# Causal linear attention without carried states, and a rearranged last expert group and final store

## The chip, the cores and the metric

One NeuronCore of a Trainium2 chip runs the whole kernel. The metric is the device time of one execution in microseconds (us), from launch to the end; lower is better. Engines are named as in the profile: PE (TensorE matmul), PEld (TensorE weight load), DVE (VectorE), ACT (ScalarE), POOL (GpSimd), SP (the queue that issues the loads).

## The reference, cut to what matters

One decoder layer over 256 tokens of 1024 features, in float32: adaptive norm, a mixer of two branches (gated linear attention and a short gated convolution), then 64 experts in 8 groups, each token going to two experts of one group, then a last RMSNorm. What the change touches is the linear attention and the last norm:

```python
b = jnp.cumsum(gc, axis=3)                    # per chunk of 64 tokens; gc = log of the forget gate
q_t = qc * jnp.exp(b); k_t = kc * jnp.exp(-b); k_s = kc * jnp.exp(b_last - b)
attn = jnp.where(causal, einsum('nbhid,nbhjd->nbhij', q_t, k_t), 0.0)
o_intra = einsum('nbhij,nbhjv->nbhiv', attn, vc)
decay = jnp.exp(b_last)[:, :, :, 0, :]
def step(state, inp):                          # scan over the 4 chunks, 4 heads
    q_i, k_i, v_i, d_i = inp
    o_i = einsum('bhid,bhdv->bhiv', q_i, state)
    state = d_i[..., None] * state + einsum('bhid,bhiv->bhdv', k_i, v_i)
    return state, o_i
o = o_intra + o_inter
...
x = x + g2 * hier_moe(h)
return rmsnorm(x, final_norm_g)
```

There are 4 heads with 128 key features and 256 value features each, and 4 chunks of 64 tokens.

## The kernel before, in words

The weights are read once, 475.8 MB in all, in a fixed order through SP. The mixer's weights come as blocks of 512 KB into a ring of 12 (class Stream): 88 blocks of the input and output projections ("win") and 48 of the modulation ("modw"). A block is freed when DVE has read it, and the free issues the next load, so the ring runs as far ahead as DVE lets it. After the last block, the same ring and the buffers that the mixer gives up take "units" of 2 MB: 8 groups of 12 units of expert weights ("ew"; for the last group's second layer "el"). A unit's buffer is freed, and the next load issued, when PE has used it.

In the mixer every weight block is split by ACT (L340, high part) and DVE (L347, low part) into two float32r halves, and PE multiplies it in three passes (L356, 24 matmuls a block, or L364 and L373 for the first 16 blocks). The splits run 5 blocks ahead of PE. DVE also reduces a modulation block against the conditioning vector (L257); the table MODS says at which block each of these falls. What else the mixer does is hung on block numbers by at, first and pre: in block b, "first" comes before the splits, "pre" after them, "at" last before the block's matmuls. Each engine works its instructions in that order.

The linear attention hangs on blocks 16 to 46. Gate values give the running sum bb; its exponentials eb, enb and ekb weight the keys and queries (k_evac, q_evac). Then, on PE: the weighted keys are transposed (L481), attention within pairs of chunks is formed with a mask that leaves out the pair's second-chunk-on-first part (L494, DVE L498), the keys by the values give what each chunk adds to the state (L506), which ACT and DVE chain into three states (L513, L515), and the output of a head is attention times values (L525) plus query times state (L529). The output is normed per head; L556 spreads the four heads' norms over partitions with a matrix P1 that holds a row of ones per head (P1 is used again for the experts' slot tables).

An expert group's 4 experts run side by side in four column groups of PE, 32 tokens each (L1048). The last group's second layer is cut into four column chunks (LASTC: 512, 256, 128, 128) so that the work behind the last weights is short. Each chunk goes through last_part: scale out of PSUM (evac_y, L1066), spread the slots back to tokens on PE (combine, L1075) and add (L1079), square and sum on ACT (L1214), then last_weigh multiplies by the last norm's gain (L1218). At the end the sums give the norm's factor (L1241 to L1244), and four stores of 256 KB write the result. LASTN says in how many pieces the load of each chunk's weights is issued.

All four chunks accumulate in one PSUM tile ps of two banks: columns 0 to 511 in the first, all others in the second. A DMA issue on SP waits for an earlier DMA: the issues of the last pieces stand on the landings of earlier ones.

The places that the change touches:

```python
first(22, gate5); first(23, gate8); at(23, gate7)
at(27, gla_kst); at(28, gla_attn); first(28, gla_kst2); pre(29, gla_attn2, 0); pre(29, gla_attn2, 1)
at(29, gla_state, 0, 1); first(30, gla_state2, 0); pre(30, gla_state2, 1); at(31, gla_state, 2); pre(32, gla_state2, 2)
at(33, gla_o, 0) ... first(34, gla_o2, 0) ... at(36, gla_ss) ... at(39, gla_ss4)
```

Of the kernel before, what the change touches and what calls it, by code (L numbers as in the profile page):

```python
# [28 lines left out]
LASTN = (2, 2, 4, 4)  # L29
# [5 lines left out]
MODS = (16, 17, 18, 19, 22, 26, 27, 28, 31, 33, 34, 35, 37, 39, 41, 43, 45, 47, 49, 51, 52, 53, 54, 55, 56, 57, 58,  # L35
# [82 lines left out]
def trunk_kernel(ctx: ExitStack, tc: tile.TileContext, xT: bass.AP, c: bass.AP, modw: bass.AP,  # L118
# [113 lines left out]
    V.memset(cmask[0:64, 64:128], 0)  # L232
# [15 lines left out]
    G.memset(P1, 0.0)  # L248
    for h in range(H):
        G.memset(P1[32 * h:32 * h + 1, h // 2, h % 2], 1.0)  # L250
# [157 lines left out]
    la, bb, eb, enb = (t9[:, i].rearrange("p (h t) -> p h t", h=H) for i in range(4))  # L408
# [3 lines left out]
    ekb, qt, kt_, ks = (gb[:, i] for i in range(4))  # L412
    decay = sm.tile([128, H, 4], F32, name="decay")
    b4 = bb.rearrange("p h (c t) -> p (h c) t", t=64)
# [37 lines left out]
    def gate5():  # L452
        S.activation(eb, bb, AF.Exp, scale=-1.0 / 16)

    def gate6():
        V.tensor_sub(ekb.rearrange("p h (c t) -> p (h c) t", t=64),
                     b4[:, :, 63:64].to_broadcast([128, 16, 64]), b4)

    def gate7():
        V.tensor_copy(decay, eb.rearrange("p h (c t) -> p h c t", t=64)[:, :, :, 63])  # L460

    def gate8():
        S.activation(enb, bb, AF.Exp, scale=1.0 / 16)
        S.activation(ekb, ekb, AF.Exp, scale=-1.0 / 16)
# [3 lines left out]
    def gla_setup():  # L468
        g2 = big.tile([128, 4, 1024], F32, name="gc", tag="T11")
        L["kst"] = g2[:, 0].rearrange("p (t d) -> p t d", t=2)  # L470
        L["at"] = g2[:, 1].rearrange("p (t h i) -> p t h i", t=2, h=H)
        for ch, i in ((1, 2), (2, 3), (3, 0)):
            L["S", ch] = g2[:, i].rearrange("p (h d) -> p h d", h=H)
        G.memset(g2[:, 1], 0.0)

    def gla_kst():
        L["pk"] = []
        for tt in range(TT):
            ps = mt(H, 128)
            for h in range(H):  # L480
                T.transpose(ps[:, h], ks[:, h, 128 * tt:128 * tt + 128], ident)  # L481
            L["pk"].append(ps)

    def gla_kst2():
        for tt in range(TT):
            S.copy(L["kst"][:, tt], fl(L["pk"][tt]))

    def gla_attn():
        L["pa"] = []
        for tt in range(TT):  # L490
# [9 lines left out]
    def gla_state(*chs):  # L500
        for ch in chs:
            L["ps", ch] = [mt(2, 256) for _ in range(2)]
# [818 lines left out]
```

## Time and profile before

| | us |
|---|---|
| median of 3 runs (lowest, highest) | 1206.16 (1203.33, 1206.17) |
| profiled execution, its own time | 1202.4 |
| its span, first to last instruction | 1200.5 |
| PE busy | 903.8 (75%) |
| DVE busy | 381.6 (32%) |
| ACT busy | 224.6 (19%) |
| HBM read | 475.79 MB, 397 GB/s over the span |
| chain that ended last | DMA 67%, PE 28%, DVE 3% |

The shares of busy time are averages over three stages: the mixer to about 292 us, the eight expert groups to about 1180 us, and the tail behind the last weights. The chain of waits says who set the time in each: PE in the mixer, the load stream in the expert groups, and a chain that hops between PE, DVE and ACT in the tail.

### The profile page before, as it was taken

To read this page: it belongs to the slowest core of one execution; us is meant where nothing else is said; L and a number is where in the kernel's file an instruction comes from. 1 tells how busy PE (TensorE), PEld (TensorE's weight loads), DVE (VectorE), ACT (ScalarE), POOL (GpSimd) and SP (SyncE) were. 2 spreads that over 40 slices of the span, in tenths; PEclk is the share of its full clock that TensorE was granted. 3 is DMA by queue.
4 is the path that set the end of the run, shared out by engine and by line. 5 is a ranking of instruction groups with operands and counts; after the bars stand their busy time and mean duration, and the time that the engine had idled before them with its cause. 6 is when DMAs were issued, how large, how long until landed. Compare 5 with 4: busy or idle time off the path is not lost.

```text
span 1200.5 us, 14607 instructions
## 1 busy us (share of the span) xinstructions
PE 903.8 (75%) x6188; PEld 476.8 (40%) x6188; DVE 381.6 (32%) x720; ACT 224.6 (19%) x375; POOL 3.9 (0%) x15
## 2 busy tenths in 40 slices
PE   9999999999888766666666667676667566756575
PEld 6999999999342212121212212121212111412112
DVE  8968699664431111111111101020202000302103
ACT  6775545443210101010101000000000000100002
POOL 0000000000000000000000000000000000000000
PEclk9999999999998888798788888788888886989888
DMA  9987589979999999999999999999999999999996
GB/s 369 396 339 254 177 300 339 381 271 364 421 430 430 429 432 431 430 431 430 430 432 430 429 432 430 430 432 429 431 431 430 431 430 431 428 432 431 429 428 261
DMA packets 51483, 477.84 MB, mean 398 GB/s; under 512 B 5971, under 2 KB 6099, under 8 KB 27093
## 3 DMA queue, kind: packets, MB, share of 16 engines
q1 hardware_dynamic: 50544, 475.81, 95.8%
q8 instruction: 50, 0.82, 0.2%
q10 hardware_dynamic: 868, 1.05, 0.2%
q14 instruction: 21, 0.16, 0.0%
HBM read 475.79 MB, written 1.05 MB: 397 GB/s over the span
## 4 chain that ended last, share of the span: by engine, by line
DMA 67%; PE 28%; DVE 3%; ACT 0%; issue 0%; DVEq 0%; SPq 0%; ACTq 0%
DMA unit<-in_ew_dram 45%; DMA ring<-in_ew_dram 19%; PE z L356 17%; PE a L1048 3%; DMA unit<-in_el_dram 2%; PE m L364 2%; PE z L373 2%; PE m L1020 1%; PE m L1075 1%; PE m L529 0%; DMA xt<-in_xT_dram 0%; PE z L220 0%; PE m L506 0%; PE m L525 0%; PE m L312 0%
## 5 line engine op out<-in xcount | busy, mean ns | idle before, releaser
L1048 PE MATMUL a<-unit,xt 128*32 128x512 f32 x1440 | 209.5, 711 | 103.9 <-DMA unit<-in_ew_dram 103.9
L1048 PE MATMUL a<-unit,gt 128*32 128x512 f32 x736 | 121.7, 799 | 63.5 <-DMA unit<-in_ew_dram 59.9
L1048 PEld LDWEIGHTS a<-unit,xt 128*32 128x32 f32 x1440 | 43.8, 120 | 248.2 <-DMA unit<-in_ew_dram 139.0
L356 PE MATMUL z<-hhl,sp 128*128 128x256 f32 x1152 | 140.9, 284 | 0.0
L356 PEld LDWEIGHTS z<-hhl,sp 128*128 128x128 f32 x1152 | 138.9, 192 | 1.6 <-issue 1.5
L1024 ACT ACTIVATE xt<-m,modc,A 128x128 f32<-128x128 f32 x64 | 25.9, 453 | 518.5 <-PE m L1020 517.4
L347 DVE TENSOR_TENSOR sp<-ring,sp 128x1024 fp32r<-128x1024 f32 x88 | 106.8, 1219 | 40.2 <-ACT sp L340 40.1
L1048 PE MATMUL a<-ring,xt 128*32 128x512 f32 x608 | 84.2, 676 | 35.9 <-DMA ring<-in_ew_dram 35.9
L340 ACT CAST sp<-ring 128x1024 fp32r<-128x1024 f32 x88 | 91.5, 1048 | 93.8 <-PE z L356 66.6
L1079 DVE TENSOR_TENSOR wk<-wk,m 128x512 f32<-128x512 f32 (+2 forms) x64 | 41.7, 654 | 194.5 <-PE m L1075 194.5
L1066 DVE TENSOR_TENSOR xt<-a,xt 128x1024 f32<-128x1024 f32 (+3 forms) x19 | 20.0, 1054 | 257.4 <-PE a L1048 249.8
L1048 PEld LDWEIGHTS a<-unit,gt 128*32 128x32 f32 x736 | 24.3, 129 | 148.6 <-DMA unit<-in_ew_dram 93.1
L1075 PE MATMUL m<-xt,pwt 128*128 128x512 f32 (+2 forms) x136 | 64.5, 617 | 5.2 <-DVE xt L1066 5.2
L1056 DVE TENSOR_TENSOR gt<-gt,a 128x512 f32<-128x512 f32 x16 | 11.0, 687 | 173.8 <-ACT gt L1055 173.8
L1020 PEld LDWEIGHTS m<-scr,wk 128*128 128x128 f32 x512 | 58.7, 192 | 19.0 <-issue 18.7
L1020 PE MATMUL m<-scr,wk 128*128 128x128 f32 x512 | 62.4, 279 | 3.7 <-DVE scr L1009 2.9
L257 DVE SCALAR_TENSOR_TENSOR xt<-ring,xt 128x1024 f32<-128x1024 f32 x48 | 58.5, 1218 | 0.6 <-DMA ring<-in_modw_dram 0.2
L1048 PEld LDWEIGHTS a<-ring,xt 128*32 128x32 f32 x608 | 18.6, 117 | 97.3 <-DMA ring<-in_ew_dram 49.3
L1026 DVE TENSOR_SCALAR xt<-m,A,modc 128x128 f32<-128x128 f32 x64 | 23.3, 405 | 103.9 <-PE m L1020 103.9
L1048 PE MATMUL a<-ring,gt 128*32 128x512 f32 x208 | 36.3, 833 | 21.8 <-DMA ring<-in_ew_dram 21.1
L1075 PEld LDWEIGHTS m<-xt,pwt 128*128 128x128 f32 x136 | 26.0, 206 | 50.3 <-issue 38.0
L1055 ACT ACTIVATE gt<-a 128x512 f32<-128x512 f32 x16 | 9.6, 597 | 182.3 <-PE a L1048 182.3
(255 smaller groups left out, 633.0 us busy)
## 6 DMA issues: line engine op xcount, KB each, us to landing
unit<-in_ew_dram SPq DMA_DIRECT2D x136, 2048.0 KB, 38.8
ring<-in_ew_dram SPq DMA_DIRECT2D x48, 2048.0 KB, 38.8
ring<-in_win_dram SPq DMA_DIRECT2D x88, 512.0 KB, 7.8
ring<-in_modw_dram SPq DMA_DIRECT2D x48, 512.0 KB, 6.8
ring<-in_ew_dram SPq DMA_DIRECT2D x12, 512.0 KB, 7.3
unit<-in_el_dram SPq DMA_DIRECT2D x4, 1024.0 KB, 31.6
ring<-in_el_dram SPq DMA_DIRECT2D x4, 512.0 KB, 20.2
unit<-in_el_dram SPq DMA_DIRECT2D x4, 512.0 KB, 11.2
```

Source lines behind the costliest of these rows:

```text
L257: V.scalar_tensor_tensor(scr, st.block("m", i, b), 1.0, cB, op0=OP.mult, op1=OP.mult, accum_out=modc[:, 4 * i + b:4 * i + b + 1])
L340: S.copy(sp(b)[:, 0], st.block("w", n, i))
L347: V.tensor_sub(t[:, 1], st.block("w", n, i), t[:, 0].bitcast(F32))
L356: T.matmul(ps, t[:, ws, k], rhs[rs][:, k], start=(clear and k == 0 and n == 0), stop=(k == KT - 1 and n == 2), skip_group_check=True)
L364: T.matmul(pb[:, h % 2], t[:, ws, h], hl[rs][:, kk], start=(kk == 0 and h % 2 == 0 and n == 0), stop=(kk == KT - 1 and h % 2 == 1 and n == ...
L373: T.matmul(pv[tt][hh], hl[rs][:, kk, 128 * tt:128 * tt + 128], t[:, ws, 512 * hh:512 * hh + 512], start=(kk == 0 and n == 0), stop=(kk == ...
L1020: T.matmul(ps[j], acc[:, tt, f:f + 128], Pm[:, tt], start=(tt == 0), stop=(tt == 1))
L1024: S.activation(xg[:, k], ps[j], AF.Identity, bias=B2[:, k:k + 1], scale=A2[:, k:k + 1])
L1026: V.tensor_scalar(xg[:, k], ps[j], A2[:, k:k + 1], B2[:, k:k + 1], op0=OP.mult, op1=OP.add)
L1048: T.matmul(ps[32 * j:32 * j + 32, 512 * hh:512 * hh + 512], lhsT[:, 32 * j:32 * j + 32], w[:, j, 512 * hh:512 * hh + 512], start=first, st ...
L1075: T.matmul(ps[:, :w], pwt[:, tt], X["y"][:, s], start=True, stop=True)
L1079: V.tensor_add(total[:, tt, s], total[:, tt, s], ps[:, :w])
```

## The change

The attention no longer keeps states. With the exponents taken from the end of a pair's first chunk (wE for the first chunk's tokens, bb for the second's), a pair of chunks needs one attention matrix of 128 by 128, and the second pair sees the first through a third matrix between keys and queries decayed to the pair's border (kd, qd, in gla_far). So the transposes of the keys, the state matmuls and the state updates go; three attention matrices stand in their place, and a head's output is two matmuls over 256 and 128 tokens for each half of the values. On the diagonal pairs the matmul of 128 by 128 is issued as two, for keys 0 to 63 and 64 to 127 (the second over the later 64 queries only). Four entries of MODS move (27, 28, 31 to 28, 29, 30). The per-head norms are spread with one row of ones each, into four banks.

In the last group the two chunks of 128 columns accumulate in a second PSUM tile, in one bank each; scaling out of PSUM stands ahead of the other DVE work; both small chunks are multiplied before either is combined; the gain's multiplication is cut and moved; the loads come in 1, 2, 2 and 4 pieces instead of 2, 2, 4 and 4; and the result is stored in five pieces, two of them of 128 KB.

On PE, around blocks 27 to 35, before (gb holds weighted keys and queries, gc the transposed keys, attention and states, t_126 the values, sp the split weights; L481 transposes, L506 states, L525 and L529 outputs):

```order
L481 MATMUL m<-ident,gb 128x128 x8
L356 MATMUL z<-hhl,sp 128x256 x24
L494 MATMUL m<-gb 128x128 x8
L356 MATMUL z<-hhl,sp 128x256 x24
L506 MATMUL m<-t_126,gc 128x256 x8
L356 MATMUL z<-hhl,sp 128x256 x48
L506 MATMUL m<-t_126,gc 128x256 x4
L356 MATMUL z<-hhl,sp 128x256 x48
L525 MATMUL m<-gc,t_126 128x128 x2
L529 MATMUL m<-gb,gc 128x64 x3
```

The last two rows come eight times, four times on each side of a block. On PE now, in the same stretch (t_120 is the values):

```order
L487 MATMUL m<-gb 64x128
L488 MATMUL m<-gb 64x64
L485 MATMUL m<-gb 128x128 x4
L352 MATMUL z<-hhl,sp 128x256 x96
L505 MATMUL m<-gc,t_120 128x256
L506 MATMUL m<-gc,t_120 128x128
```

The first two rows come eight times, the last two eight times in two lots. The transposes and states are gone, the 96 matmuls of four blocks stand in one piece where before other work stood between them.

On DVE, from the last group's first scaling out of PSUM to the sum of squares, before (L1066 scales, L1079 adds a chunk for each half of the tokens, L1218 multiplies by the gain, L1241 adds the sums of squares):

```order
L1066 TENSOR_TENSOR xt<-a,xt 128x512
L1079 TENSOR_TENSOR wk<-wk,m 128x512 x2
L1218 TENSOR_TENSOR wk<-wk 128x2x512
L1066 TENSOR_TENSOR xt<-a,xt 128x256
L1079 TENSOR_TENSOR wk<-wk,m 128x256 x2
L1218 TENSOR_TENSOR wk<-wk 128x2x256
L1066 TENSOR_TENSOR xt<-a,xt 128x128
L1079 TENSOR_TENSOR wk<-wk,m 128x128 x2
L1218 TENSOR_TENSOR wk<-wk 128x2x128
L1066 TENSOR_TENSOR xt<-a,xt 128x128
L1079 TENSOR_TENSOR wk<-wk,m 128x128 x2
```

And now (L1177 scales, L1047 adds, L1193 multiplies by the gain):

```order
L1177 TENSOR_TENSOR xt<-a,xt 128x512
L1047 TENSOR_TENSOR wk<-wk,m 128x512 x2
L1177 TENSOR_TENSOR xt<-a,xt 128x256
L1193 TENSOR_TENSOR wk<-wk 128x512
L1047 TENSOR_TENSOR wk<-wk,m 128x256 x2
L1193 TENSOR_TENSOR wk<-wk 128x512
L1177 TENSOR_TENSOR xt<-a,xt 128x128
L1193 TENSOR_TENSOR wk<-wk 128x2x256
L1177 TENSOR_TENSOR xt<-a,xt 128x128
L1047 TENSOR_TENSOR wk<-wk,m 128x128 x4
```

Each scaling has moved ahead of the gain's multiplication that stood before it, and the four adds of the small chunks stand together at the end.

On SP, the last loads and the stores, as one piece of the difference:

```order
-L107 DMA unit<-in_el_dram 128x2048 x4
-L107 DMA ring<-in_el_dram 128x1024 x4
+L107 DMA unit<-in_el_dram 128x4096
+L107 DMA unit<-in_el_dram 128x2048 x2
+L107 DMA ring<-in_el_dram 128x2048 x2
 L107 DMA unit<-in_el_dram 128x1024 x4
```

Three issues fewer stand ahead of the last four, whose size is unchanged.

The diff, cut to its core:

```diff
-LASTN = (2, 2, 4, 4)
+LASTN = (1, 2, 2, 4)
...
-MODS = (16, 17, 18, 19, 22, 26, 27, 28, 31, 33, 34, 35, 37, 39, 41, 43, 45, 47, 49, 51, 52, 53, 54, 55, 56, 57, 58,
+MODS = (16, 17, 18, 19, 22, 26, 28, 29, 30, 33, 34, 35, 37, 39, 41, 43, 45, 47, 49, 51, 52, 53, 54, 55, 56, 57, 58,
...
-    V.memset(cmask[0:64, 64:128], 0)
...
-    la, bb, eb, enb = (t9[:, i].rearrange("p (h t) -> p h t", h=H) for i in range(4))
+    la, bb, eq, ek = (t9[:, i].rearrange("p (h t) -> p h t", h=H) for i in range(4))
...
+    def half(t, c):
+
+        return t.rearrange("p h (a c t) -> p (h a) c t", c=2, t=64)[:, :, c]
...
     def gate5():
-        S.activation(eb, bb, AF.Exp, scale=-1.0 / 16)
+
+        V.tensor_sub(wE, half(bb, 0)[:, :, 63:64].to_broadcast([128, 8, 64]), half(bb, 0))
 
     def gate6():
-        V.tensor_sub(ekb.rearrange("p h (c t) -> p (h c) t", t=64),
-                     b4[:, :, 63:64].to_broadcast([128, 16, 64]), b4)
-
-    def gate7():
-        V.tensor_copy(decay, eb.rearrange("p h (c t) -> p h c t", t=64)[:, :, :, 63])
-
-    def gate8():
-        S.activation(enb, bb, AF.Exp, scale=1.0 / 16)
-        S.activation(ekb, ekb, AF.Exp, scale=-1.0 / 16)
+        for d, sg in ((ek, -1.0), (eq, 1.0)):
+            S.activation(half(d, 0), wE, AF.Exp, scale=sg / 16)
+            S.activation(half(d, 1), half(bb, 1), AF.Exp, scale=-sg / 16)
+        for c in range(2):
+            S.activation(decay[:, c], bb[:, :, 64 * c + 127], AF.Exp, scale=-1.0 / 16)
...
+    def gla_far():
+        for d, x, c, o in ((kd, kx, 0, 0), (qd, qx, 1, 128)):
+            V.tensor_mul(d, x[:, :, o:o + 128], decay[:, c, :, None].to_broadcast([128, H, 128]))
+
+    def gla_attn():
+        L["pa"] = []
+        a, b = slice(0, 128), slice(128, 256)
+        for k, q in ((kx[:, :, a], qx[:, :, a]), (kx[:, :, b], qx[:, :, b]), (kd, qd)):
             ps = mt(H, 128)
             for h in range(H):
-                T.matmul(ps[:, h], kt_[:, h, s], qt[:, h, s], start=True, stop=True)
+                if k is kd:
+                    T.matmul(ps[:, h], k[:, h], q[:, h], start=True, stop=True)
+                    continue
+                T.matmul(ps[0:64, h], k[:, h, 0:64], q[:, h], start=True, stop=True, skip_group_check=True)
+                T.matmul(ps[64:128, h, 64:128], k[:, h, 64:128], q[:, h, 64:128], start=True, stop=True,
+                         skip_group_check=True)
             L["pa"].append(ps)
 
-    def gla_attn2(tt):
-        V.copy_predicated(L["at"][:, tt], cmask[:, None, :].to_broadcast([128, H, 128]), L["pa"][tt])
...
+    def gla_near(tt):
+        t, ps = (L["at0"][:, :, 0:128], L["at1"])[tt], L["pa"][tt]
+        for n, c in ((64, 0), (128, 64)):
+            V.copy_predicated(t[:n, :, c:c + 64], cmask[:n, None, c:c + 64].to_broadcast([n, H, 64]), ps[:n, :, c:c + 64])
+
+    def gla_cross():
+        S.copy(L["at0"][:, :, 128:256], L["pa"][2])
 
     def gla_o(h):
...
-            for tt in range(TT):
-                s = slice(128 * tt, 128 * tt + 128)
-                T.matmul(ps[:, a, s], vt[:, tt, f:f + 128], L["at"][:, tt, h],
-                         start=(a == 0 and tt == 0), stop=False, skip_group_check=True)
-            for ch in range(1, 4):
-                s = slice(64 * ch, 64 * ch + 64)
-                T.matmul(ps[:, a, s], L["S", ch][:, h, 128 * a:128 * a + 128], qt[:, h, s],
-                         start=False, stop=(a == 1 and ch == 3), skip_group_check=True)
+            T.matmul(ps[:, a], vt[:, 0, f:f + 128], L["at0"][:, h], start=(a == 0), stop=False, skip_group_check=True)
+            T.matmul(ps[:, a, 128:256], vt[:, 1, f:f + 128], L["at1"][:, h], start=False, stop=(a == 1),
+                     skip_group_check=True)
...
-            T.matmul(L["rso"][h // 2][:, h % 2], P1[:, h // 2, h % 2], scr2, start=True, stop=True)
+            r = slice(32 * h, 32 * h + 1)
+            T.matmul(L["rso"][h], onesf[r], scr2[r], start=True, stop=True)
...
+    at(27, gla_far)
     at(40, st.free, "T12")
...
+    at(29, gla_attn)
+    first(31, gla_cross)
+    pre(31, gla_near, 0)
+    pre(31, gla_near, 1)
...
     def k_evac(j):
         s = slice(2 * j, 2 * j + 2)
-        V.tensor_mul(ks[:, s], pk[j], ekb[:, s])
-        V.tensor_mul(kt_[:, s], pk[j], enb[:, s])
+        V.tensor_mul(kx[:, s], pk[j], ek[:, s])
...
+    ps2 = pa.tile([128, D], F32, name="a")
+    LASTP = (ps[:, 0:512], ps[:, 512:768], ps2[:, 0:128], ps2[:, 512:640])
...
-    last_weigh(0)
-    last_part(1)
+    last_evac(1)
+    last_weigh(0, 512, 0, 1)
+    last_sums(1)
+    last_weigh(0, 512, 1, 2)
...
+    for n in (2, 3):
+        for f in range(4):
+            last_mm(n, w[:, n - 2, f], f)
+        if n == 2:
+            last_evac(2)
+    last_weigh(512, 256)
+    last_evac(3)
+    last_sums(2)
+    last_sums(3)
...
+    put(V, nc.sync, 0, 0, 512)
+    put(S, S, 1, 0, 512)
+    put(V, nc.sync, 0, 512, 1024)
+    put(S, S, 1, 512, 768)
+    put(V, nc.sync, 1, 768, 1024)
```

## Rows read from the trace of the kernel before

**Rows 1.** The page, 40 slices: DMA busy share in tenths.

```profile
DMA  9987589979999999999999999999999999999996
```

**Rows 2.** The chain that ended last: start us, length us, what.

```profile
64.23 1.73 PE z L430 x8
...
106.85 5.95 PE z L356 x48
...
120.66 0.45 PE m L525 x4
121.11 0.62 PE m L529 x6
...
150.06 109.43 PE z L356 x912
...
374.28 37.96 DMA unit<-in_ew_dram
```

**Rows 3.** Windows, us: busy by engine, granted clock, DMA share, GB/s.

```profile
120.00:150.00 30.00, 29.94 (x255) 28.84 (x254) 18.09 (x27) 15.86 (x23) 0.00 (x0) 1.00 0.55 176
150.00:180.00 30.00, 30.00 (x252) 30.00 (x251) 29.40 (x48) 13.55 (x17) 0.00 (x0) 1.00 0.87 301
180.00:210.00 30.00, 30.00 (x252) 30.00 (x251) 29.42 (x43) 16.33 (x20) 0.00 (x0) 1.00 0.94 339
400.00:1150.00 750.00, 491.92 (x3028) 150.90 (x3029) 106.92 (x236) 39.55 (x87) 0.00 (x0) 0.85 1.01 431
1197.00:1198.00 1.00, 0.00 (x0) 0.00 (x0) 0.00 (x0) 0.00 (x0) 0.00 (x0) 0.50 1.06 408
```

**Rows 4.** Timeline, attention: start, length, engine, line, shapes, [idle <-releaser].

```profile
65.61 29.14 PE L356 MATMUL z<-hhl,sp 128*128 128x256 f32 x240
...
94.59 1.04 PE L481 MATMUL m<-ident,gb 128*128 128x128 f32 x8
...
104.86 1.99 PE L506 MATMUL m<-t,gc 64*128 64x256 f32 x14 [1.08 <-DVE gc L498]
...
112.73 1.99 PE L506 MATMUL m<-t,gc 64*128 64x256 f32 x8
...
114.65 5.81 PEld L356 LDWEIGHTS z<-hhl,sp 128*128 128x128 f32 x48 [0.33 <-issue]
...
132.22 5.99 PE L356 MATMUL z<-hhl,sp 128*128 128x256 f32 x48
```

**Rows 5.** Timeline, the spread of the four norms.

```profile
148.10 1.97 PE L556 MATMUL m<-scr,P 128*128 128x256 f32 x8
```

**Rows 6.** DVE groups between 84 and 133 us: count | busy us, mean ns.

```profile
L515 DVE SCALAR_TENSOR_TENSOR gc<-gc,decay,m 128x256 f32<-128x256 f32 x8 | 3.3, 473 | 0.0
```

**Rows 7.** Timeline, the tail behind the last weights.

```profile
1184.95 0.27 PEld L1200 LDWEIGHTS a<-ring,gt 128*32 128x32 f32 x8 [0.16 <-DMA ring<-in_el_dram]
...
1186.56 0.42 DVE L1066 TENSOR_TENSOR xt<-a,xt 128x256 f32<-128x256 f32 x1
...
1188.09 1.08 PE L1200 MATMUL a<-unit,gt 128*32 128x128 f32 x32
...
1190.78 0.51 DVE L1079 TENSOR_TENSOR wk<-wk,m 128x128 f32<-128x128 f32 x2 [0.58 <-PE m L1075]
...
1191.10 0.31 ACT L1214 ACTIVATE wk<-wk 128x128 f32<-128x128 f32 x1 [1.83 <-DVE wk L1079]
...
1192.32 0.28 DVE L1066 TENSOR_TENSOR xt<-a,xt 128x128 f32<-128x128 f32 x1
...
1194.27 0.16 DVE L1241 TENSOR_REDUCE rs<-ssq 128x2 f32<-128x8 f32 x1
...
1195.95 0.88 SPq L1252 DMA_DIRECT2D out_dram<-wk  x2
```

**Rows 8.** The last piece of the last load: issue, and time to landing.

```profile
L107 SPq DMA_DIRECT2D unit<-in_el_dram x1: 328/328/328, 1180.0 to 1180.0; - x1
DMA to landing us min/median/max: 9.9/9.9/9.9
```

More of the change, by code (lines that the diff above doesn't have):

```diff
@@ L497, in gla_attn2 @@
-    def gla_attn2(tt):
-        V.copy_predicated(L["at"][:, tt], cmask[:, None, :].to_broadcast([128, H, 128]), L["pa"][tt])
-    def gla_state(*chs):
-        for ch in chs:
-            L["ps", ch] = [mt(2, 256) for _ in range(2)]
-        for h in range(H):
-            for ch in chs:
-                tt, r = ch // 2, slice(64 * (ch % 2), 64 * (ch % 2) + 64)
-                T.matmul(L["ps", ch][h // 2][:, h % 2], L["kst"][r, tt, 128 * h:128 * h + 128],
-                         L["v"][r, tt, 256 * h:256 * h + 256], start=True, stop=True)
@@ L509, in gla_state2 @@
-    def gla_state2(ch):
-        new = L["S", ch + 1]
-        for h in range(H):
-            if ch == 0:
-                S.copy(new[:, h], L["ps", ch][h // 2][:, h % 2])
-            else:
-                V.scalar_tensor_tensor(new[:, h], L["S", ch][:, h], decay[:, h, ch:ch + 1],
-                                       L["ps", ch][h // 2][:, h % 2], op0=OP.mult, op1=OP.add)
+                if k is kd:
+                    T.matmul(ps[:, h], k[:, h], q[:, h], start=True, stop=True)
+                    continue
@@ L613, in trunk_kernel @@
     at(20, gate4)
-    at(21, gate6)
-    first(22, gate5)
-    first(23, gate8)
-    at(23, gate7)
+    at(21, gate5)
+    first(22, gate6)
     at(23, lambda: k_evac(0))
@@ L1248, in trunk_kernel, with put @@
-    S.activation(total[:, 1, lo], total[:, 1, lo], AF.Copy, scale=rs[:, 1:2])
-    S.dma_start(out[128:256, lo], total[:, 1, lo])
-    for tt in range(TT):
-        V.tensor_scalar(total[:, tt, hi], total[:, tt, hi], rs[:, tt:tt + 1], None, op0=OP.mult)
-        nc.sync.dma_start(out[128 * tt:128 * tt + 128, hi], total[:, tt, hi])
+    def put(e, q, tt, c0, c1):
+        t, r = total[:, tt, c0:c1], rs[:, tt:tt + 1]
+        if e is S:
+            S.activation(t, t, AF.Copy, scale=r)
+        elif c0 == 768:
+            V.scalar_tensor_tensor(t, t, r, fgr[:, c0:c1], op0=OP.mult, op1=OP.mult)
+        else:
+            V.tensor_scalar(t, t, r, None, op0=OP.mult)
+        q.dma_start(out[128 * tt:128 * tt + 128, c0:c1], t)
```

93 lines of the change are left out of this document (29 added, 64 removed).

## The prediction

> **What bounds the kernel now.** I read the page's slices first, then the chain of waits, then the windows, then the timelines of the two places that the change touches. The slices show that the DMA engines are full from about 300 us on, and have holes before that [rows 1]. The chain names who makes the holes: from 106.85 us on it stays on PE's attention and block matmuls, 109.43 us of them in one piece from 150.06, and at 374 us it goes over to the loads of the expert weights [rows 2]. From 400 to 1150 us DMA is at 1.01 and 431 GB/s [rows 3]: nothing in that stretch can be hastened by an engine. But the stream can begin earlier. Between 120 and 150 us DMA is at 0.55 with PE at 29.94 of 30 [rows 3], since ring blocks come free only as fast as PE works off the split weights. So time taken out of PE's row in the mixer shifts every later free, and with it the whole stream. Behind the last weights there is a tail of its own.
>
> **PE in the attention, before.** PE's work up to block 27 ends where the transposes start, at 94.59, and the last output matmul ends where the block matmuls go on at 132.22 [rows 4]: 37.6 us. Of these, 168 are passes of weight blocks (24, 24, 48, 48 and, between the two lots of outputs, 24). One pass is 29.14 / 240 = 0.121 us [rows 4], so 20.4 us are blocks and 17.2 us the attention with its gaps: the wait of 1.08 us for the mask on DVE, and 0.33 us of issue after the state matmuls [rows 4].
>
> **PE in the attention, after.** A float32 matmul shows as two passes. A pass over 256 columns takes 1.73 / 8 = 0.216 us, one over 128 columns 0.45 / 4 = 0.112, and one over 64 columns with 128 weights 0.62 / 6 = 0.103 [rows 2], so a short pass is bound by its weights. The outputs are now 8 matmuls over 256 and 8 over 128 columns: 16 x 0.216 + 16 x 0.112 = 5.2 us. The far attention is 8 passes of 0.112: 0.9 us. The two near ones are 16 passes over 128 columns and 16 over 64, each with 64 weights, on the two column halves of the array. One after another with full weight time they take 16 x 0.112 + 16 x 0.103 = 3.4 us; side by side 16 x 0.112 = 1.8 us. That halves can run side by side is seen in the state matmuls: 14 passes with both row halves in use take 1.99 us, and 8 with one half take as much [rows 4]. In the last group 32 passes with 32 weights each, on four column groups, take 1.08 us, 0.034 each [rows 7]. I take 2.4 us, nearer to side by side. With 0.33 us on leaving the narrow shape the attention costs 8.8 us instead of 17.2: 8.4 us less; between 7.4 (all one after another) and 9.4 (side by side, no gap).
>
> The Trainium skill, "TensorE: Matmul & The Clock Gate", section "LDWEIGHTS (loading the stationary operand)", says that a weight load takes its number of columns over 1.2 GHz, whatever the depth. For 128 weights that is 0.107 us, and the trace agrees with 0.103. For 64 weights it gives 0.053 us, and by it the near attention would take 2.6 us even one after another; the sum would move by 0.2 us.
>
> The spread of the norms was 1.97 us for 8 passes [rows 5]. It now uses one row of the array for each head, in four different row groups and four banks. It stays at 1.97 if they don't overlap, and falls to about 0.9 (8 weight loads of 0.112) if they do. I take 0.7 us less, from 0 to 1.1. Sum on PE: 9.1 us less, from 7.4 to 10.5.
>
> **What hides the rest.** On DVE the chained states go (3.3 us [rows 6]), two key products, half of one subtraction and a small copy; two products for the far part and two more mask copies come, in sum about 3.8 us less. Could DVE then not follow a faster PE? Between 120 and 150 us it was idle for 30 - 18.09 = 11.9 us [rows 3], more than the 9.1 us that PE gains, and its own work falls as well. Its splits are five blocks, some 14 us, ahead. The new work that PE waits for is the far products at block 27 and the masks at block 31: each is called two blocks before PE needs it, 5.8 us, behind one split and one reduction. If that cover is gone, the price is the old wait, 1.08 us. ACT loses copies and gains two small exponentials; it costs nothing while the splits run ahead. The moved modulation blocks only change which of three ring blocks comes free a block earlier. POOL, which loses the memsets of P1, is busy for 3.9 us in all on the page. The loads at 120 to 150 us have 45% of DMA to spare for a faster PE.
>
> **The tail.** The last piece of the last load is issued at 1180.0 and lands 9.9 us later, at 1189.9 [rows 8]. Its size is unchanged, and I take its landing as fixed relative to the stream. Before, PE was not waiting for it: the chunks queued behind one another, and the last scaling out of PSUM started only at 1192.32 [rows 7]. Now the matmuls of both small chunks are issued before either is combined. So the first thing to be late is the landing itself. Chunk 1's load comes in two pieces, so half of its passes, not a quarter, start when the second has landed (1184.95 [rows 7]): its scaling starts at about 1186.0 instead of 1186.56, and the small chunks are ready in time for the landing. From 1189.9, half of a chunk's passes (0.54 us of 1.08 [rows 7]) end at 1190.45, and the last scaling starts at 1190.5, 1.8 us earlier. From there to the sum of squares it was 1.95 us (1192.32 to 1194.27 [rows 7]). Now the other small chunk's combination stands in front on PE, with its pair of adds (0.51) and its squares (0.31 each), mostly beside the last chunk's: I add 0.15. That is 1.65 us less. If the larger pieces ahead are issued earlier and the landing moves up, the chunks' own work sets the time, up to 2.8 us less; if none of the second chunk's work is hidden (0.5 + 0.6 us), 0.7 us less.
>
> The stores move the same 1 MB, at 408 GB/s [rows 3] about 2.6 us, and the third issue on SP comes as late as before (0.88 us for two issues [rows 7]); ACT's second comes some 0.2 us behind it but is half as long. I take 0, with 0.4 us either way. The Trainium skill, "DMA: Bandwidth & Descriptors", section "Bandwidth", speaks against small pieces: it has 138 GB/s for 64 KB and 341 GB/s for 1 MB. An estimate from it for two pieces of 128 KB would be 0.5 us more in all, if nothing else were in flight; no row here shows a lone small store.
>
> Sum: 9.1 + 1.65 = 10.75 us, from 7.4 + 0.3 to 10.5 + 3.2. On the profiled execution, 1202.4 us, that gives 1191.6; on the median of the runs, 1206.16, it gives 1195.4. The profiled one is the fastest of four, so I take a time between, nearer to the median: 1194.5 us.
>
> **Rivals.** A difference under 0.3% (3.6 us) can't be told from none in this kernel.
> 1. *The narrow matmuls don't overlap and PE drains between the halves.* For it: 0.33 us of issue after the state matmuls [rows 4]. Against: 0.034 us a pass in the last group. Price: 16 changes of half at 0.33 us, 5.3 us: 1194.5 + 5.3 = about 1200. The Trainium skill, "TensorEngine Tiling (Array Packing)", section "Tiling Modes", says that a change of tiling mode drains the array, a change of tile not. The halves are tiles of one mode; the trace agrees as far as it shows a gap only on leaving.
> 2. *DVE becomes the bound.* For it: 29.40 and 29.42 us of 30 from 150 to 210 us [rows 3]; if it sets the pace there, PE's gain is lost before 210 us and only the tail is left: 1206.2 - 1.7 = 1204.5, no difference that can be told. Against: PE is at 30.00 in the same windows, and the chain is PE's throughout.
> 3. *The landing moves up.* The gain in the tail becomes 2.8 us: about 1193.
> 4. *Slower: TensorE's clock falls in the mixer.* The granted clock is 1.00 in all windows to 210 us, and 0.85 where PE waits for loads [rows 3]. If the new attention lets it fall to 1.2 GHz, PE's work there costs twice. The gain is used up once 10.75 us of work run at the lower level; 15 us give 1206.2 - 10.75 + 15 = 1210. Against: the new attention has fewer gaps than the old, whose wait of 1.08 us left the clock at 1.00.
>
> **How the numbers follow.** My forecast has 0.74 (1190 to 1199), rival 1 has 0.08, rival 2 0.08, rival 3 0.06, the slower one 0.04. Faster by over 0.3% means below 1202.5: the forecast, rival 3 and most of rival 1, 0.87. Rival 2 with the rest of rival 1 makes 0.09 for no difference; slower 0.04. The range reaches from the forecast's low end, 1189.5, to rival 1's time, 1200.5, and leaves rivals 2 and 4 out.
>
> **What would show it.** In the changed profile: no transposes and no state matmuls between blocks 27 and 33, and the block matmuls after the last output at about 124 instead of 132.2; the 32 short passes within 1.8 to 3.4 us; the chain on PE up to about 365 instead of 374 us; the last landing at about 1181; the sum of squares 2.6 to 2.8 us behind that landing instead of 4.4. If the block matmuls go on 8 us earlier but the last landing doesn't, I am wrong about the stream; if the splits on DVE end later than PE wants them between 150 and 210 us, rival 2 is right.

## The result, and the profile after

The changed kernel takes 1191.81 us (median of 4 runs, 1191.36 to 1192.36), the kernel before in the same comparison 1204.91 us (median of 4, 1203.33 to 1206.17). The ratio is 0.9892, with a 95% interval from 0.9875 to 0.9909: 13.1 us less, between 11.0 and 15.1. The forecast was 1194.5 us, in a range from 1189.5 to 1200.5. The profiled execution of after took 1191.47 us with a span of 1189.5.

The page's line of DMA slices, which answers to [rows 1]:

```profile
DMA  9988689979999999999999999999999999999996
```

The hole between 90 and 150 us (the fourth and fifth slice) is smaller, 8 and 6 tenths instead of 7 and 5; the rest is as before. The chain of waits (start us, length us, what; [rows 2]):

```profile
115.56 0.43 PE m L505 x2
...
118.19 2.87 PE z L352 x24
...
140.02 109.65 PE z L352 x912
249.85 17.32 PE z L352 x144
...
355.96 32.10 DMA ring<-in_ew_dram
```

The long piece of block matmuls starts at 140.02 instead of 150.06, and the chain goes over to the loads at 355.96 instead of 374.28. That last difference, 18 us, is more than the whole gain; experiments 6 and 7 show what it is worth.

The timeline of PE and its weight loads (PEld) in the attention; columns as in [rows 4], which it answers, the last row as [rows 5]:

```profile
101.00 0.32 PE L487 MATMUL m<-gb 128*64 128x128 f32 x1
...
102.89 0.97 PEld L485 LDWEIGHTS m<-gb 128*128 128x128 f32 x8 [0.17 <-DVE sp L343]
102.89 1.16 PE L485 MATMUL m<-gb 128*128 128x128 f32 x8
103.81 11.76 PE L352 MATMUL z<-hhl,sp 128*128 128x256 f32 x96
...
123.44 5.99 PE L352 MATMUL z<-hhl,sp 128*128 128x256 f32 x48
...
139.31 0.71 PE L532 MATMUL m<-scr,onesf 1*128 1x256 f32 x8
```

No transposes and no state matmuls are left. The two near heads' lots, 32 short passes, run from 101.00 to 102.89, and the far ones to about 103.8. The outputs come in two lots, the first from 115.56 to 118.19 in the chain above, 2.63 us, and the block matmuls go on at 123.44 instead of 132.22. The spread of the norms takes 0.71 us instead of 1.97.

Windows, columns as in [rows 3]. First before, from 100 to 300 us:

```profile
100.00:300.00 200.00, 198.80 (x1629) 193.99 (x1628) 145.45 (x223) 88.82 (x125) 0.00 (x0) 1.00 0.84 300
```

then after, with three of the windows of [rows 3]:

```profile
100.00:300.00 200.00, 198.90 (x1657) 190.53 (x1660) 145.93 (x235) 90.72 (x128) 0.00 (x0) 1.00 0.88 321
...
300.00:400.00 100.00, 83.58 (x616) 33.04 (x608) 30.81 (x99) 15.11 (x36) 0.00 (x0) 0.93 1.01 429
...
120.00:150.00 30.00, 29.94 (x252) 28.51 (x252) 24.36 (x37) 16.47 (x23) 0.00 (x0) 1.00 0.68 218
150.00:180.00 30.00, 30.00 (x252) 30.00 (x251) 29.79 (x45) 16.66 (x21) 0.00 (x0) 1.00 0.89 315
180.00:210.00 30.00, 30.00 (x252) 30.00 (x251) 28.47 (x41) 14.33 (x17) 0.00 (x0) 1.00 0.99 382
```

This is where the time came from. PE is full in both kernels, but between 100 and 300 us after moves 321 GB/s instead of 300: 21 GB/s x 200 us = 4.2 MB more. From 0 to 100 us it moves 0.3 MB less (354 against 357 GB/s), from 300 to 400 us 0.2 MB more (429 against 427), so at 400 us it is 4.1 MB ahead. From 400 to 1150 us both streams run at 430 or 431 GB/s with a DMA share of 1.01; at that rate 4.1 MB are 9.5 us. The last load's last piece (its issue and its time to landing, as [rows 8]):

```profile
L107 SPq DMA_DIRECT2D unit<-in_el_dram x1: 328/328/328, 1165.4 to 1165.4; - x1
...
DMA to landing us min/median/max: 14.7/14.7/14.7
```

It lands at 1165.4 + 14.7 = 1180.1 instead of 1189.9: 9.8 us earlier, close to what those megabytes say. Behind it stands the tail, the answer to [rows 7]:

```profile
1177.92 1.08 PE L1172 MATMUL a<-unit,gt 128*32 128x128 f32 x32
...
1179.41 0.38 PEld L1172 LDWEIGHTS a<-unit,gt 128*32 128x32 f32 x16 [0.68 <-DVE xt L1177]
1180.19 0.38 PEld L1172 LDWEIGHTS a<-unit,gt 128*32 128x32 f32 x16 [0.40 <-DMA unit<-in_el_dram]
...
1180.90 0.29 DVE L1177 TENSOR_TENSOR xt<-a,xt 128x128 f32<-128x128 f32 x1 [0.95 <-PE a L1172]
1181.29 0.99 DVE L1047 TENSOR_TENSOR wk<-wk,m 128x128 f32<-128x128 f32 x4
...
1182.77 0.16 DVE L1220 TENSOR_REDUCE rs<-ssq 128x2 f32<-128x8 f32 x1 [0.15 <-ACT wk L1189]
...
1184.01 1.32 SPq L1233 DMA_DIRECT2D out_dram<-wk  x3
```

The first half of the last chunk's passes is done ahead of the landing, and the second half waits 0.40 us for it: now the landing is what comes last. The reduction of the sums of squares stands 2.58 us behind the landing (1182.77 - 1180.19), where it stood 4.37 us behind it (1194.27 - 1189.9). From there to the end of the span it takes 6.73 us, 0.50 more than before (1200.5 - 1194.27 = 6.23): the five stores are a little dearer than four.

### The profile page after: what moved, and what is told of

It reads as the page before. It is cut to its first block, busy times and chain, and to the rows that moved or that the text cites. A ratio compares the mean times of both kernels' runs of the same rounds, so it can differ in the third digit from the quotient of the medians.

```text
span 1189.5 us, 14476 instructions
## 1 busy us (share of the span) xinstructions
PE 889.5 (75%) x6132; PEld 469.2 (39%) x6132; DVE 376.8 (32%) x712; ACT 222.9 (19%) x374; POOL 2.8 (0%) x11
## 4 chain that ended last, share of the span: by engine, by line
DMA 69%; PE 28%; DVE 2%; ACT 0%; issue 0%; ACTq 0%; SPq 0%; DVEq 0%
DMA unit<-in_ew_dram 46%; DMA ring<-in_ew_dram 19%; PE z L352 17%; DMA unit<-in_el_dram 4%; PE a L1016 3%; PE m L360 2%; PE z L369 2%; PE m L988 1%; PE z L220 0%; PE m L1043 0%; PE m L292 0%; PE m L505 0%; PE m L308 0%; PE m L654 0%; DVE P L1004 0%
## 5 line engine op out<-in xcount | busy, mean ns | idle before, releaser
L1016 PE MATMUL a<-unit,xt 128*32 128x512 f32 x1440 | 205.2, 699 | 99.0 <-DMA unit<-in_ew_dram 98.9
L1047 DVE TENSOR_TENSOR wk<-wk,m 128x512 f32<-128x512 f32 (+2 forms) x64 | 41.7, 654 | 186.2 <-PE m L1043 186.1
L1034 DVE TENSOR_TENSOR xt<-a,xt 128x1024 f32<-128x1024 f32 x15 | 18.4, 1223 | 252.7 <-PE a L1016 252.7
L1043 PE MATMUL m<-xt,pwt 128*128 128x512 f32 (+2 forms) x136 | 61.3, 593 | 2.7 <-DVE xt L1177 1.4
```

Source lines behind the costliest of these rows:

```text
L1016: T.matmul(ps[32 * j:32 * j + 32, 512 * hh:512 * hh + 512], lhsT[:, 32 * j:32 * j + 32], w[:, j, 512 * hh:512 * hh + 512], start=first, st ...
L1043: T.matmul(ps[:, :w], pwt[:, tt], X["y"][:, s], start=True, stop=True)
L1047: V.tensor_add(total[:, tt, s], total[:, tt, s], ps[:, :w])
```

## The experiments

The theory: before 300 us the ring blocks come free at the pace of PE's row, so PE time taken out of the mixer moves the whole weight stream by as much; behind the last landing the new order saves about 1.3 us net. The rivals: the gain comes from elsewhere in the attention (buffers, DVE), or mostly from the tail or from the cut of the last loads.

The moment at which the mixer starts differs between profiles by more than a microsecond without a change in the code ahead of it: PE's first matmuls of the gates (16 passes over 256 columns with 32 weights) start at 60.10 us in before, at 60.66 in after, and between 59.69 and 60.94 in the experiments. Where landings are compared below, they are counted from that row ("from the gates"): 1129.8 us before, 1119.5 after, 10.3 us less. The two rows, before and after:

```profile
60.10 1.07 PE L420 MATMUL z<-t,e 128*32 128x256 f32 x16
```

```profile
60.66 1.07 PE L422 MATMUL z<-t,e 128*32 128x256 f32 x16
```

**1. The attention alone** (tail, cuts of the last loads and stores as before).

```diff
-LASTN = (1, 2, 2, 4)
+LASTN = (2, 2, 4, 4)
-    ps2 = pa.tile([128, D], F32, name="a")
-    LASTP = (ps[:, 0:512], ps[:, 512:768], ps2[:, 0:128], ps2[:, 512:640])
...
-    def last_mm(n, w, f):
+    def last_mm(c0, cw, w, f):
...
+            T.matmul(ps[32 * j:32 * j + 32, c0:c0 + cw], gT[:, f, 32 * j:32 * j + 32], w[:, j],
```

> The new attention with the last group, the loads and the stores of the kernel before. Theory (time taken out of PE's row in the mixer shifts the whole load stream one for one): the block matmuls go on about 9 us earlier after the outputs and about 9.8 us earlier after the spread of the norms, the last load lands at about 1180 instead of 1189.9, the sum of squares follows it by 4.4 us as before, span about 1190.8, time about 9.7 us under the kernel before. Rival (DVE or the loads set the pace in the mixer): PE waits between 150 and 210 us, the last landing stays at 1189.9, span about 1200.5. Rival (half and half, PE's gain partly given back while the first expert groups fill up): landing at about 1185.

1193.52 us against 1204.22, ratio 0.9916 (0.9900 to 0.9933): 10.7 us less. The last landing (1170.7 + 9.9) is 1119.9 us from the gates, within half a microsecond of after's; the reduction stands 4.4 us behind it, as in before, and the end 6.2 us behind that.

**2. The tail alone** (attention as before).

```diff
-LASTN = (2, 2, 4, 4)
+LASTN = (1, 2, 2, 4)
...
+    ps2 = pa.tile([128, D], F32, name="a")
+    LASTP = (ps[:, 0:512], ps[:, 512:768], ps2[:, 0:128], ps2[:, 512:640])
```

> The old attention with the new last group, load pieces and five stores. Theory (the last landing is fixed relative to the stream, the tail behind it is shorter): last landing at 1189.9 as before, the sum of squares 2.7 us behind it instead of 4.4, the stores 0.5 us longer, span about 1199.2, time 1.2 us less, no difference that the timing can tell. Rival (larger pieces issued earlier let the last load land earlier): landing at 1187 or before, span 1196 to 1197.

1201.75 us against 1204.22, ratio 0.9984 (0.9975 to 0.9994): 2.5 us less by the medians, 1.9 by the ratio, whose interval means 0.7 to 3.0. In the timeline of its tail (columns as above)

```profile
1190.34 0.38 PEld L1204 LDWEIGHTS a<-unit,gt 128*32 128x32 f32 x16 [0.39 <-DMA unit<-in_el_dram]
...
1192.92 0.16 DVE L1252 TENSOR_REDUCE rs<-ssq 128x2 f32<-128x8 f32 x1
```

the landing is where it was before (1130.0 us from the gates) and the reduction 2.58 us behind it. So the two parts are separate, and the product of their ratios, 0.9900, lies inside the interval of after's 0.9892 (0.9875 to 0.9909): the attention gives about four fifths.

**3. Four stores instead of five.** The last two become one of 256 KB, scaled on DVE in two steps.

```diff
-    put(S, S, 1, 512, 768)
-    put(V, nc.sync, 1, 768, 1024)
+    V.tensor_scalar(t[:, 512:768], t[:, 512:768], r, None, op0=OP.mult)
+    V.scalar_tensor_tensor(t[:, 768:1024], t[:, 768:1024], r, fgr[:, 768:1024], op0=OP.mult, op1=OP.mult)
+    nc.sync.dma_start(out[128:256, 512:1024], t[:, 512:1024])
```

> The changed kernel with the last two stores made one of 256 KB on SP, so four stores of 256 KB, and DVE doing all of the second half's last 512 columns. Theory (the fifth store, issued late by ACT behind two activations, lands last and sets the end): from the sum of squares to the end 6.3 us instead of 6.7, time 0.3 to 0.4 us less. Rival (five pieces cost nothing, the bytes set the end): 6.7 us and no change, or longer, since DVE works 0.3 us more before the last issue.

1191.94 us, ratio 0.9900 (0.9884 to 0.9917): no difference from after. From the reduction (1183.11) to the end of the span (1189.6) it is 6.49 us, 0.24 less than with five, and between the 6.3 of the theory and the 6.7 of the rival. A likely reason, not tried by itself: the second scaling step on DVE in front of the one large store nearly costs what the fifth store does, for the large one is issued at

```profile
1185.39 0.33 SPq L1241 DMA_DIRECT2D out_dram<-wk  x1
```

2.28 us behind the reduction, where after's last issue (ACT's second, at 1185.21) starts 2.44 us behind it.

**4. The near attention whole:** one matmul with 128 weights for each head instead of two column halves with 64.

```diff
...
-                T.matmul(ps[0:64, h], k[:, h, 0:64], q[:, h], start=True, stop=True, skip_group_check=True)
-                T.matmul(ps[64:128, h, 64:128], k[:, h, 64:128], q[:, h, 64:128], start=True, stop=True,
-                         skip_group_check=True)
+                T.matmul(ps[:, h], k[:, h], q[:, h], start=True, stop=True)
```

> The changed kernel with each near attention matrix formed by one matmul of 128x128 per head instead of two on 64 columns (what the mask drops is computed as well). Theory (the 32 short passes run side by side and so cost no more than 16 full ones): 16 passes of 0.107 us, 1.7 us instead of 1.9, and no gap on leaving; time within 0.3 us. Rival (the halves save PE time, since half of each near matrix isn't needed): PE 0.8 us or more longer in that place.

1191.67 us, ratio 0.9898 (0.9882 to 0.9915): the same. In PE's timeline all 24 passes, near and far, stand as one group:

```profile
99.94 2.84 PE L484 MATMUL m<-gb 128*128 128x128 f32 x24
102.54 11.76 PE L352 MATMUL z<-hhl,sp 128*128 128x256 f32 x96
```

2.60 us from the first to the next block matmul, where after needs 2.81 (101.00 to 103.81). The halves leave out a quarter of the arithmetic and save nothing; in PE's row they cost 0.2 us. That is a gap on leaving them: in after the weight loads stand idle for 0.17 us in front of the far part (the bracket at 102.89), and so they do in every other run with halves. The profile puts this gap to a split on DVE, but experiment 4 speaks against that:

```profile
99.82 2.77 PEld L484 LDWEIGHTS m<-gb 128*128 128x128 f32 x24
100.64 1.22 DVE L343 TENSOR_TENSOR sp<-ring,sp 128x1024 fp32r<-128x1024 f32 x1
```

Its 24 weight loads run through without a gap, and the 17th, the first of the far part, starts at about 101.6 (an estimate: two thirds of the way from 99.82 to the next block's first load at 102.51), while the same split is still at work.

**5. The norms spread as before, by P1** (8 passes of 128 rows in one row group, still into four banks; POOL's memsets of P1 are back too).

```diff
-            r = slice(32 * h, 32 * h + 1)
-            T.matmul(L["rso"][h], onesf[r], scr2[r], start=True, stop=True)
+            T.matmul(L["rso"][h], P1[:, h // 2, h % 2], scr2, start=True, stop=True)
```

> The kernel after, with the norms spread as before by the matrices P1: 8 passes with 128 rows in one row group (1.97 us before) instead of one row of the array for each head in four row groups (0.71 us), still into four banks. Theory (the four row groups run side by side, and PE's row counts one for one): the group takes 1.8 to 2.0 us and the time is 1.0 to 1.4 us longer, about 1193. Rival 1 (the four banks made it short): the group stays at 0.7 to 0.9 us and the time at 1191.8. Rival 2 (the group gets longer, but the wait behind it gives it back): 1.9 us in the group, no difference in time.

1193.45 us, ratio 0.9916 (0.9900 to 0.9933). Three other variants on the same chip (in experiments 6, 7 and 8) come to 1191.4 to 1191.5: 2.0 us more, with an uncertainty as large. The group

```profile
139.07 1.97 PE L534 MATMUL m<-scr,P 128*128 128x256 f32 x8
```

takes exactly its old time, so the four banks weren't what made it short, and the last landing comes 1.5 us later from the gates than in after (1166.6 + 14.8 - 60.43 = 1121.0 against 1119.5). The theory holds; rival 1 falls by the group, rival 2 by the landing. Not all of the 2.0 us is the spread's, though: in this run's profile the reduction stands 3.4 us behind the landing (1184.78 - 1181.4) where after's stands 2.58. TensorE's granted clock was at the lower of its two levels, 1.2 GHz (0.50), all through the 5 us from 1165, after a wait of 2.98 us for a load that ended at 1161.78; in after its mean there was 0.66. Here and in after:

```profile
1165.00:1170.00 5.00, 2.99 (x16) 1.28 (x20) 0.69 (x1) 2.58 (x4) 0.00 (x0) 0.50 1.01 427
```

```profile
1165.00:1170.00 5.00, 4.48 (x24) 1.03 (x24) 0.00 (x0) 1.71 (x3) 0.00 (x0) 0.66 1.02 425
```

The first chunk's passes then end 7.4 us ahead of the landing instead of 8.8, and the small chunks are no longer ready when it comes.

**6. The same 9.9 us of PE work at three places.** In the mixer at block 36:

```diff
+    def busy():
+        d = zt(512)
+        for _ in range(23):
+            T.matmul(d[:, 0:256], ident, xres[:, 0], start=True, stop=True)
+        rot["z"] += 3
+    at(36, busy)
```

> The kernel after, with 23 matmuls of 128x256 float32 into a PSUM tile that nobody reads, put into PE's row at block 36 of the mixer: 46 passes x 0.216 us = 9.9 us of TensorE work that the result does not use. Theory (every microsecond in PE's row before 350 us moves the whole stream of expert weights): the chain of waits stays on PE for 9 to 10 us longer, the last weights land 9 to 10 us later, and the time is 1201 to 1202 us, as with the old attention and the new tail (1201.75). Rival (the gain came from something else in the attention, such as fewer buffers held or less work on DVE, and PE's row alone is worth little): under 2 us more, 1192 to 1194 us.

1201.43 us, ratio 0.9985 (0.9975 to 0.9994). Nearly the whole gain is gone, with the new attention in place: it is 10.0 us more than the 1191.4 to 1191.5 of the variants on the same chip.

```profile
128.41 10.09 PE L602 MATMUL z<-xt,ident 128*128 128x256 f32 x46
...
148.30 0.71 PE L532 MATMUL m<-scr,onesf 1*128 1x256 f32 x8
```

The spread of the norms stands at 148.30 as in before (148.10, [rows 5]), and between 100 and 300 us

```profile
100.00:300.00 200.00, 199.66 (x1626) 194.03 (x1626) 142.89 (x219) 88.66 (x122) 0.00 (x0) 1.00 0.83 302
```

the stream is back at 302 GB/s. The last piece lands at 1188.1,

```profile
1188.15 0.38 PEld L1180 LDWEIGHTS a<-unit,gt 128*32 128x32 f32 x16 [0.44 <-DMA unit<-in_el_dram]
```

1128.3 us from the gates (59.81): 8.8 us later than in after, in a profiled execution that was the fastest of the ten (1199.45). PE's row did it; for buffers, DVE and the moved modulation blocks, which are here as in after, no more than about 1 us is left.

The same matmuls in the fourth group of experts, where PE has time to spare:

```diff
+            if g == 3 and u == 6:
+                d = mt()
+                for _ in range(23):
+                    T.matmul(d[:, 0:256], ident, P1[:, 0].rearrange("p t k -> p (t k)"), start=True, stop=True)
```

> The kernel after, with the same 23 matmuls (9.9 us of TensorE work that the result does not use) put into the fourth group of experts instead of the mixer. Theory (from 400 us on the DMA stream alone sets the time and PE waits for it): nothing, within 1 us of the kernel after (1191.8). Rival (PE's work counts wherever it stands): 1201 to 1202 us. It shows whether 9.9 us of PE work cost something because they are work or because of where they stand.

1191.49 us, ratio 0.9900 (0.9883 to 0.9917): nothing, as the theory has it.

**7. The same work at 320 us,** in the first group of experts, behind the second gate's transposes: after the DMA engines have filled up, but where the chain of waits still stands on PE (it leaves PE at 355.96 in after).

```diff
                     gate2_rows()
+                    d = mt()
+                    for _ in range(23):
+                        T.matmul(d[:, 0:256], ident, P1[:, 0].rearrange("p t k -> p (t k)"), start=True, stop=True)
```

> The kernel after, with the same 23 matmuls (9.9 us of TensorE work that the result does not use) in the first group of experts, behind the transposes of the second gate at about 320 us. Theory A (the stretch in which PE's row counts ends where the DMA engines become full, at 300 us): under 1.5 us more than the kernel after, 1191.5 to 1193.3 us. Theory B (it ends where the chain of waits leaves PE, at about 356 us): 9 to 10 us more, 1201 to 1202 us, as in the mixer.

1191.40 us, ratio 0.9899 (0.9884 to 0.9915): nothing. The chain of this kernel

```profile
321.73 10.62 PE m L1160 x46
...
375.73 27.20 DMA unit<-in_ew_dram
```

names the added work as a part of what ended last, 10.62 us long, and stays on PE to 375.73; the time knows nothing of it. The windows tell it rightly:

```profile
100.00:300.00 200.00, 198.89 (x1657) 190.46 (x1659) 145.85 (x235) 90.81 (x128) 0.00 (x0) 1.00 0.88 321
300.00:400.00 100.00, 88.41 (x630) 41.68 (x626) 30.79 (x99) 14.85 (x35) 0.00 (x0) 0.94 1.01 429
```

The stream ran at 429 GB/s all the while, whatever PE did. So PE's row counts at 128 us (experiment 6) and no longer at 321 us, where the DMA engines are full (a share of 1.01 from 300 to 400 us); at which moment between the two it stops counting was not tried.

**8. The last group's loads cut as before.**

```diff
-LASTN = (1, 2, 2, 4)
+LASTN = (2, 2, 4, 4)
```

> The kernel after, with the last group's loads cut as before, (2, 2, 4, 4) pieces a chunk instead of (1, 2, 2, 4). Theory (the landing of the last weights is set by the stream, and the pieces only change when an issue is made): the last landing within 0.5 us of the kernel after, at 1180 us, chunk 1 ready a little earlier, and the time within 1 us of 1191.8. Rival (larger pieces are issued earlier and bring the landing forward): 1 to 2 us later, 1193 to 1194 us.

1191.40 us, ratio 0.9901 (0.9885 to 0.9918), the last landing 1119.7 us from the gates against 1119.5. The pieces of the last loads make no difference that can be told.

**9. Chunk 2 combined between the halves of chunk 3.**

```diff
-    for n in (2, 3):
-        for f in range(4):
-            last_mm(n, w[:, n - 2, f], f)
-        if n == 2:
-            last_evac(2)
+    for f in range(4):
+        last_mm(2, w[:, 0, f], f)
+    for f in range(2):
+        last_mm(3, w[:, 1, f], f)
+    last_evac(2)
+    last_sums(2)
     last_weigh(512, 256)
+    for f in range(2, 4):
+        last_mm(3, w[:, 1, f], f)
     last_evac(3)
-    last_sums(2)
     last_sums(3)
```

> The kernel after, with the two small chunks taken in another order: chunk 2's combination on PE stands between the first half of chunk 3's passes and the second, which wait for the last landing, instead of behind both. Theory (from the last landing on everything counts, and chunk 2's combination fits into the 0.4 us in which PE waits for the landing): the reduction of the sums 2.0 to 2.3 us behind the last landing instead of 2.6, the time 0.3 to 0.6 us shorter, about 1191.4, too little to be told by the time. Rival (chunk 2's work isn't on the path behind the landing): still 2.6 us.

1192.90 us, ratio 0.9912 (0.9898 to 0.9925); by the medians 1.1 us worse than after, which the intervals don't separate, and 1.5 us worse than experiment 7's kernel on the same chip, all of whose runs (up to 1191.80) are shorter than all of these (from 1192.11). Its tail:

```profile
1179.99 0.71 PE L1043 MATMUL m<-xt,pwt 128*128 128x128 f32 x4 [0.41 <-DVE xt L1177]
1180.63 0.64 PE L1172 MATMUL a<-unit,gt 128*32 128x128 f32 x16
1181.88 0.71 PE L1043 MATMUL m<-xt,pwt 128*128 128x128 f32 x4 [0.61 <-DVE xt L1177]
```

The last load's last piece lands at 1165.3 + 14.8 = 1180.1, and the second half of chunk 3's passes starts only at 1180.63: chunk 2's combination waits for its own scaling, which now comes behind chunk 3's first half, and so doesn't fit into the gap ahead of the landing. On DVE a weighing of 0.69 us then stands in front of the last scaling, at 1181.54 instead of 1180.90, and the reduction comes at 1183.35, 3.2 us behind the landing. The theory of this run fell: the order is no better. It doesn't show what chunk 2's work costs where after has it, for the edit also puts chunk 2's adds on DVE in front of that weighing, which in after is done ahead of the landing (from 1179.27).

**10. That order, the whole near matmuls and the old cuts together:** the edits of experiments 4, 8 and 9 in one kernel.

```diff
-LASTN = (1, 2, 2, 4)
+LASTN = (2, 2, 4, 4)
...
+                T.matmul(ps[:, h], k[:, h], q[:, h], start=True, stop=True)
...
+    for f in range(2):
+        last_mm(3, w[:, 1, f], f)
+    last_evac(2)
+    last_sums(2)
```

> The kernel after, with that order of the small chunks, the near attention as one whole matmul for each head, and the last group's loads cut as in the kernel before. Theory: the gains of the three are 0.3 to 0.6 us, 0.2 us and none, and add up to 0.5 to 0.8 us: 1191.0 to 1191.3 us. Rival: no difference from the kernel after, 1191.8 us.

1192.22 us, ratio 0.9907 (0.9892 to 0.9922): no better, and the forecast gain of 0.5 to 0.8 us isn't there. The reduction stands 3.2 us behind the landing (1183.40 - 1180.2), as in experiment 9. No version tried beats after by more than the measurement can tell.

## Why the prediction was right, step by step

**The stream.** The prediction's mechanism, PE's row in the mixer sets when ring blocks come free and so where the stream stands, is shown three ways: the long piece of block matmuls starts 10.0 us earlier (150.06 and 140.02), 10.6 us counted from the gates, the last landing comes 10.3 us earlier from there, and 9.9 us of idle work put in at block 36 takes 9.6 us of it away again by the medians (1201.43 against 1191.81; 8.8 us by the landing of its profile). The sum was 9.1 us (7.4 to 10.5); what it was short of are two terms:
- The near attention took 1.89 us (101.00 to 102.89), the gap on leaving it included, where 2.4 and 0.33 were taken. It runs side by side, the low end of the bounds, and the gap is 0.17 us.
- The spread of the norms gained 1.26 us where 0.7 was taken; this is a little more than the upper bound of 1.1, which had counted 8 weight loads of 0.112 us.

The Trainium skill, "TensorEngine Tiling (Array Packing)", section "Tiling Modes", says that a change of tiling mode drains the array. In after's timeline of the weight loads

```profile
103.78 11.58 PEld L352 LDWEIGHTS z<-hhl,sp 128*128 128x128 f32 x96
...
130.36 8.69 PEld L352 LDWEIGHTS z<-hhl,sp 128*128 128x128 f32 x72 [0.41 <-issue]
...
139.95 1.12 PEld L352 LDWEIGHTS z<-hhl,sp 128*128 128x128 f32 x9 [0.33 <-issue]
```

the kernel leaves 32-column tiles with a gap of 0.41 us and one-row tiles with 0.33, and none stands at 103.78, where the shape stays the same; the 64-column halves it leaves with the 0.17 us that experiment 4 is without. The trace agrees with the page, and the gap differs from shape to shape: the prediction had taken the 0.33 us of another one.

**The tail.** 1.65 us were forecast up to the sum of squares, from 4.4 to 2.6 or 2.8 us behind the landing; it is 2.58, 1.8 us less, in after and in the tail alone. The landing was named as the first thing to be late, and PE's wait for it [0.40] shows it. The first half of the last chunk's passes waits for chunk 2's scaling out of PSUM (its weight loads stand idle for 0.68 us), which the prediction didn't have; it ends ahead of the landing and costs nothing. The two chunks' banks are halves of one tile; that this makes the wait is likely, but wasn't tried by itself.

**The stores.** The term of 0 was mis-sized: 0.50 us more from the reduction to the end, just outside the bound of 0.4. In the trace it is the later last issue, 2.44 us behind the reduction instead of 2.15 (1196.42 - 1194.27), and its landing 3.1 us later: half the length didn't help, for the 256 KB stores land in 2.5 and 3.0 us. The prediction's estimate from the Trainium skill, "DMA: Bandwidth & Descriptors", section "Bandwidth", whose table is of loads, was 0.5 us for the two small pieces, and the size agrees. How much of it the size of the pieces costs isn't shown: one piece of 256 KB in their place, behind a second scaling step, ends 0.24 us sooner (experiment 3).

So 10.3 + 1.8 - 0.5 = 11.6 us stand against 10.75 forecast; the profiled executions differ by 10.9 us (1202.4 and 1191.47), with the later start of 0.57 us in it, the medians by 13.1 (11.0 to 15.1). In the later comparisons, where before ran 9 or 13 times, it stands 12.0 to 12.6 us above the variants that time like after (experiments 3, 4, 6, 7 and 8). What these are more than the sum of the terms, no run explains.

**What was choice and luck.** The time of 1194.5 us rests on a base of about 1205.25, chosen between before's profiled execution (1202.4) and its median (1206.16); the median came out at 1204.91, so the choice was lucky, and the time is still 2.7 us too long because the gain was more. A range of 11 us is a weak test. The strong ones are the signs: block matmuls at about 124 (123.44), the landing at about 1181 (1180.1), the sum of squares 2.6 to 2.8 us behind it (2.58). Two figures of the prediction don't agree with themselves: the attention side by side and without a gap gives 17.2 - 5.2 - 0.9 - 1.8 = 9.3 us, not 9.4, and the forecast's low end stands as 1190 and as 1189.5. Neither bears on the result.

**The rivals.** 1 (no overlap, 16 drains): 32 passes in 1.89 us leave no room for them; there is one gap, of 0.17 us, on leaving. 2 (DVE becomes the bound): DVE is at 29.79 of 30 us from 150 to 180 us, but PE is at 30.00 there and the gain arrives whole. 3 (the landing moves up with the larger pieces): experiment 8 shows none of it. 4 (the clock): the granted clock is 1.00 up to 300 us, as before.

**What was read wrongly.** "The chain on PE up to about 365 instead of 374 us" was given as a sign. It stands at 355.96 in after and at 375.73 in experiment 7, whose time is the same: the place where the chain changes over between 300 and 380 us says nothing here, because the loads run at 429 GB/s all through that stretch, whichever engine the chain stands on. The sign that holds is the rate of the stream before 300 us.

## What to carry to other kernels

Where a stream of loads is full from some moment to the end, count the megabytes that have moved by that moment: their difference, divided by the full rate, is the gain, and work behind that moment can be free even where the chain of waits still names it, as here. The same idle work put at two or three places brackets the moment in as many runs. In a tail behind the last landing, do everything that doesn't need it first on the engine that will wait for it, and look at what that puts in front of the last chunk on the other engines.

## What the runs showed of the hardware

- One-row matmuls, one head to each of four row groups and banks: 8 passes over 256 columns in 0.71 us, 0.089 each, against 0.246 each with 128 rows into the same four banks.
- Column halves of 64 weights run side by side but bring nothing over whole matmuls: 32 passes in 1.89 us, 0.17 us of it the gap on leaving them, against 16 of 128 weights in about 1.7 (2.60 less the far part's 0.9).
- The stream does not stay full up to its last landing: in the last 5 us the DMA share is 0.47 in after and 0.43 in before.

```profile
1175.00:1180.00 5.00, 4.00 (x72) 2.28 (x68) 3.35 (x7) 1.74 (x6) 0.00 (x0) 1.00 0.47 193
```

```profile
1185.00:1190.00 5.00, 2.85 (x52) 1.70 (x44) 3.09 (x6) 1.41 (x6) 0.00 (x0) 1.00 0.43 173
```

The first is after, the second before; the last issue was made 14.7 and 9.9 us ahead of the landing, so an issue 4.8 us earlier changed little. What would change it was not tried.
